# Two projection steps moved ahead of the first back step in even chunks of an mLSTM kernel

## The chip, the cores and the metric

The kernel runs on one core of a Trainium2 chip. The metric is the device time of one execution in microseconds (us). Before the change it is 3157.75 us, the median of three runs between 3157.44 and 3160.65 us.

The core's engines run side by side, each through its own queue in order: PE (matrix multiply, with PEld for its weight loads), DVE (vector), ACT (scalar), POOL (GpSimd) and SP, which here only issues transfers. They wait for each other through semaphores.

## The reference

One layer of a decoder: a norm, one input projection, two groups of heads that read the same projected input (a pooling mixer and an mLSTM), an output projection, a residual and a final norm. Width 1024, sequence 4096, all in float32. The change lies in the mLSTM branch, whose part that matters here is:

```python
xc = jax.nn.silu(causal_conv(mx, conv_w, conv_b))        # mx: a slice of u @ w_in, 1024 wide
q, k, v = headwise(xc, w_q), headwise(xc, w_k), headwise(mx, w_v)
gates = concatenate([q, k, v]) @ w_if + b_if             # input and forget gate of 4 heads
# chunks of 128 positions; (C, n, m) is carried from chunk to chunk
W = exp(d_log - m_t) * (q k^T)                           # within the chunk, causal
num = W v + inter * (C q);  den = sum(W) + inter * (n q)
h = num / max(|den|, exp(-m_t))
C_new = decay * C + sum(w * v k^T);  n_new = decay * n + sum(w * k)
```

## The kernel before

Every float32 matrix product that needs full precision is made of three products of a high and a low half: `split` (L109 to L111) makes the high half on ACT (L110) and the low half, the rest, on DVE (L111); `mm3` (L113 to L119) issues the three matmuls of each pair (L117 high by high, L118 high by low, L119 low by high). Lines L117 to L119 therefore stand for every such product, and the tile names tell them apart: `acc` in the mLSTM stage is the projection to `mx`.

The program has three stages: the norm and the pooling branch (L383 to L575), the mLSTM (L579 to L956), and the remaining projections (L961 on). In the middle one the sequence runs in 32 chunks of 128 positions, `n` = 0 to 31. Each turn of the loop at L935 takes the *front* of chunk n, the *back* of chunk n-1, and a share of the *projection* for a later block of 256 positions, which two chunks (an even and an odd one) share. All three are Python generators, and one `step` of a generator issues the instructions up to its next `yield`:

- `front` (L730), 13 steps: the v product from `mx` (three steps, L740), two steps for q (L750, copied by ACT at L752), two for the scores (L761), two transposes (L770), the gates (L774 to L785), the scans (L790 to L803), the split of a row into three bf16 parts (L812 to L815) and its spread over the partitions on PE (L817), and a last step with the exponentials (L820, L825, L829), the causal mask on POOL (L830), the product `dm` on DVE (L832), its split into `st` (called `wt` in the code, L833), and the scaled queries `qi` (L838 on DVE, L840 on ACT, L841 on POOL).
- `back` (L845), 13 steps with the preparing one: per head, the numerator from `st` (L867, three matmuls, of which the third needs the low half of `st`) and from the carried state (L871), the split of the state into `cs` (L643 on ACT, L644 on POOL), the division (L876 to L885), and two state updates (L896 on PE, L897 on DVE).
- `project` (L692): L702 and L703 split the four pieces of `u` on ACT and POOL; each of the 16 steps after that issues 12 matmuls (`proj_part`, L594), and each fourth step ends a pair of column groups: ACT copies `acc` to `mx` and scales it (L716, L721), POOL sets the three columns of overlap (L715, L717).

The pair's convolution is finished in pieces by `tail` (L651): six operations of DVE (L656), then the three activations of a SiLU (L678 to L680) and a product (L681). `acc` has a single PSUM buffer (L583), `mm` three, `map` four, the pieces of `u` twelve tiles (L580), `mx` five.

What is issued in which order comes from `ORDER` (L31): one string for even chunks and one for odd ones, with f for a step of the front, b of the back, p of the projection and c of a tail. This is the order of the program's text; the framework that places instructions on the engines keeps what depends on each other in order and may shift what doesn't, so the order on an engine is not that of the letters everywhere.

Of the kernel before, what the change touches and what calls it, by code (L numbers as in the profile page):

```python
# [27 lines left out]
TB = 256  # L28


ORDER = ("ffffbbffbpbffbpffppccbbbcbfpbfbbpppccc", "ffffbbbfpfffpbfbfppbccbbccfpbfpbppbbcc")  # L31
VA = P + 1
GW = P + 8

# [26 lines left out]
def tile_hybrid(  # L61
# [517 lines left out]
    with tc.tile_pool(name="b_one", bufs=1) as one, \  # L579
# [355 lines left out]
        for n in range(NB * NCH + 1):  # L935
            fr = Steps(front(n, n % 2, *xin), 13) if n < NB * NCH else None
            turn = {"f": fr, "b": bk, "p": proj}
            for what in ORDER[n % 2]:
                if what == "c":
# [275 lines left out]
```

## Time and profile before

| what | us |
|---|---|
| median of three runs | 3157.75 |
| the profiled execution, its time | 3153.02 |
| its span, first to last instruction | 3151.3 |
| PE busy with matmuls over the span | 2919.7 |
| DVE, ACT, POOL busy over the span | 2089.8, 1373.6, 960.7 |
| mean granted TensorE clock | 0.964 |

The page divides the span by lines and engines; a line such as L117 is met in all three stages, so the stages have to be looked at apart. The mLSTM stage begins at 767 us; its loop is in a steady rhythm from 873 to 1660 us, with one pair of chunks every 58.1 us. Times below are microseconds from the span's start. In a row of the timeline, the first number is the start, the second the time from the first to the last end of the instructions merged into the row, then engine, line, operation, tiles, and how many; brackets hold the idle time before it and what ended it.

### The profile page before, as it was taken

What the parts mean: (1) busy time and instruction counts of PE and PEld (TensorE: products, weight loads), DVE (VectorE), ACT (ScalarE), POOL (GpSimd) and SP (SyncE); (2) the same over time, 40 slices, a digit from 0 to 9 for tenths busy, and PEclk for the clock granted to TensorE, in tenths of its full rate; (3) what the DMA queues carried; (4) which work ended last, traced back from release to release, by engine and by line L of the source; (5) the groups of instructions that cost most, each with busy time, mean ns of one, the idle gap of its engine ahead of it and who ended that gap; (6) DMA issues with size and microseconds to landing.
All of it is one profiled execution on the core that took longest, in us unless ns stands there. A gap on an engine that the chain in (4) does not pass through costs nothing. (4 is left out here: it accounts for less than half of the span.)

```text
span 3151.3 us, 45085 instructions
## 1 busy us (share of the span) xinstructions
PE 2919.7 (93%) x15912; PEld 2522.1 (80%) x15912; DVE 2089.8 (66%) x4160; ACT 1373.6 (44%) x2727; POOL 960.7 (30%) x1015
## 2 busy tenths in 40 slices
PE   7999999996989999999997788999998899998998
PEld 6888888885989989989897566887777688876887
DVE  6555555544578878888888553566667766575666
ACT  4222122211577677767666311235556633342332
POOL 1122333333245455445445432001111145321000
PEclk9999999998899999999998899999999999998999
DMA  6344455556121121111113688765666788786654
GB/s 211 124 153 159 155 181 184 184 174 201 46 64 51 48 68 48 61 55 51 61 58 111 227 309 268 238 225 192 209 218 230 260 273 302 260 290 208 213 208 157
DMA packets 256419, 530.55 MB, mean 168 GB/s; under 512 B 28352, under 2 KB 71872, under 8 KB 256192
## 3 DMA queue, kind: packets, MB, share of 16 engines
q1 hardware_dynamic: 223936, 410.21, 37.6%
q10 hardware_dynamic: 32256, 117.45, 11.9%
q8 instruction: 125, 2.05, 0.3%
q14 instruction: 102, 0.84, 0.1%
HBM read 334.63 MB, written 192.94 MB: 167 GB/s over the span
## 5 line engine op out<-in xcount | busy, mean ns | idle before, releaser
L117 PE MATMUL acc<-u,w 128*128 128x512 f32 (+1 forms) x2016 | 691.6, 343 | 2.2 <-ACT u L110 1.8
L119 PE MATMUL acc<-u,w 128*128 128x512 f32 (+1 forms) x2016 | 682.4, 339 | 0.0
L118 PE MATMUL acc<-u,w 128*128 128x512 f32 (+1 forms) x2016 | 680.7, 338 | 0.0
L117 PE MATMUL ps<-w,sr 128*128 128x512 f32 x1344 | 536.7, 399 | 44.4 <-ACT sr L110 29.6
L119 PE MATMUL ps<-w,sr 128*128 128x512 f32 x1344 | 533.6, 397 | 9.2 <-DVE sr L111 9.0
L118 PE MATMUL ps<-w,sr 128*128 128x512 f32 x1344 | 532.5, 396 | 0.0
L111 DVE TENSOR_TENSOR sr<-sr 128x1024 fp32r<-128x1024 f32 x224 | 293.5, 1314 | 304.3 <-ACT sr L110 299.4
L110 ACT CAST sr<-sr 128x1024 fp32r<-128x1024 f32 x224 | 234.2, 1048 | 552.0 <-PE ps L118 293.6
L117 PEld LDWEIGHTS acc<-u,w 128*128 128x128 f32 x2016 | 383.7, 190 | 44.3 <-ACT u L110 2.5
L118 PEld LDWEIGHTS acc<-u,w 128*128 128x128 f32 x2016 | 383.7, 190 | 40.3
L119 PEld LDWEIGHTS acc<-u,w 128*128 128x128 f32 x2016 | 383.5, 190 | 40.2
L117 PEld LDWEIGHTS ps<-w,sr 128*128 128x128 f32 x1344 | 257.9, 192 | 99.6 <-ACT sr L110 32.3
L119 PEld LDWEIGHTS ps<-w,sr 128*128 128x128 f32 x1344 | 257.1, 191 | 69.5 <-DVE sr L111 16.7
L118 PEld LDWEIGHTS ps<-w,sr 128*128 128x128 f32 x1344 | 257.6, 192 | 53.5 <-issue 0.5
L656 DVE SCALAR_TENSOR_TENSOR xc<-mx,col,xc 128x256 f32<-128x256 f32 x384 | 221.2, 632 | 55.4 <-POOL mx L715 46.4
L644 POOL TENSOR_TENSOR cs<-c,cs 128x516 fp32r<-128x516 f32 x124 | 176.4, 1422 | 204.2 <-ACT cs L643 181.7
L1038 POOL TENSOR_TENSOR rs<-rs,nhalf 128x2 f32<-128x2 f32 x64 | 56.0, 876 | 521.0 <-DVE mv L1035 325.9
L117 PE MATMUL ps<-sr,w 128*128 128x512 f32 x448 | 176.5, 394 | 4.3 <-ACT sr L110 3.3
L118 PE MATMUL ps<-sr,w 128*128 128x512 f32 x448 | 176.0, 393 | 1.4 <-DVE sr L111 1.4
L119 PE MATMUL ps<-sr,w 128*128 128x512 f32 x448 | 175.7, 392 | 0.0
L867 PE MATMUL mm<-va,st 128*128 128x258 f32 x384 | 85.6, 318 | 64.2 <-DVE st L111 42.6
L322 DVE TENSOR_TENSOR ch<-ps,ch 128x512 f32<-128x512 f32 x192 | 127.2, 681 | 14.4 <-PE ps L119 13.6
(211 smaller groups left out, 5192.8 us busy)
## 6 DMA issues: line engine op xcount, KB each, us to landing
sr<-us_d ACTq DMA_DIRECT2D x112, 512.0 KB, 5.0
us_d<-st SPq DMA_DIRECT2D x64, 512.0 KB, 2.7
sr<-yp_d ACTq DMA_DIRECT2D x56, 512.0 KB, 5.3
sr<-ym_d ACTq DMA_DIRECT2D x56, 512.0 KB, 4.5
st<-in_x_t_dram SPq DMA_DIRECT2D x32, 512.0 KB, 6.1
yp_d<-sg SPq DMA_DIRECT2D x64, 256.0 KB, 2.5
st<-us_d SPq DMA_DIRECT2D x32, 512.0 KB, 5.8
st<-yp_d SPq DMA_DIRECT2D x32, 512.0 KB, 5.8
```

The costliest lines, as they stand in the source:

```text
L110: nc.scalar.copy(out=hi, in_=raw)
L111: (eng or nc.vector).tensor_tensor(out=lo, in0=raw, in1=hi.bitcast(F32), op=ALU.subtract)
L117: nc.tensor.matmul(ps, lhsT=a[0], rhs=b[0], start=start and k == 0, stop=False, skip_group_check=skip)
L118: nc.tensor.matmul(ps, lhsT=a[0], rhs=b[1], start=False, stop=False, skip_group_check=skip)
L119: nc.tensor.matmul(ps, lhsT=a[1], rhs=b[0], start=False, stop=stop and k == n - 1, skip_group_check=skip)
L322: nc.vector.tensor_tensor(out=v(t), in0=ps, in1=v(t), op=ALU.add)
L644: nc.gpsimd.tensor_tensor(out=t[:, 1], in0=cst[h], in1=t[:, 0].bitcast(F32), op=ALU.subtract)
L656: nc.vector.scalar_tensor_tensor(out=a[:, t], in0=m[:, t, i:i + TB], scalar=conv_w[:, jj * 4 + i:jj * 4 + i + 1], in1=a[:, t], op0=ALU.mul ...
L867: nc.tensor.matmul(nps, lhsT=wt[:, w, h, :], rhs=vh[v], start=i == 0, stop=first and i == 2)
L1038: nc.gpsimd.tensor_tensor(out=rs, in0=rs, in1=nhalf[:, 0:2], op=ALU.pow)
```

## The change

One of the two strings changes, that for even chunks. Two steps of the projection now come directly after the first four of the front, before the first of the back; in exchange the one between the third and fourth step of the back goes, and of the three at the end, two are left. The sum of letters is the same, and the string for odd chunks is not touched.

```diff
-ORDER = ("ffffbbffbpbffbpffppccbbbcbfpbfbbppppccc", "ffffbbbfpfffpbfbfppbccbbccfpbfpbppbbcc")
+ORDER = ("ffffppbbffbbffbpffppccbbbcbfpbfbbppccc", "ffffbbbfpfffpbfbfppbccbbccfpbfpbppbbcc")
```

On the engines this moves instructions in three places, the same in every pair of the steady rhythm.

The first is PE at the head of an even chunk, from the front's first q product on (`map`: the front; `mm`: the back; `acc`: the projection). Before:

```order
L750 MATMUL map<-xc,bqk 128x128 x4
L867 MATMUL mm<-va_11209,st 128x258
L867 MATMUL mm<-va_11210,st 128x258
L896 MATMUL mm<-va_11209,ws 128x258
L896 MATMUL mm<-va_11210,ws 128x258
L896 MATMUL mm<-va_11209,ws 128x258
L896 MATMUL mm<-va_11210,ws 128x258
L117 MATMUL acc<-u,w_5551 128x256
L118 MATMUL acc<-u,w_5551 128x256
L867 MATMUL mm<-va_11209,st 128x258
L871 MATMUL mm<-cs,qi 128x258 x6
```

With the change 18 matmuls of the projection stand between the q product and the first L867 (12 with the weights w_5551 and w_5552, then six with w_5553 and w_5554, of which the last are shown):

```order
L119 MATMUL acc<-u,w_5552 128x256
L117 MATMUL acc<-u,w_5553 128x256
L118 MATMUL acc<-u,w_5553 128x256
L119 MATMUL acc<-u,w_5554 128x256
L117 MATMUL acc<-u,w_5553 128x256
L118 MATMUL acc<-u,w_5553 128x256
L119 MATMUL acc<-u,w_5554 128x256
L867 MATMUL mm<-va_11209,st 128x258
L867 MATMUL mm<-va_11210,st 128x258
L867 MATMUL mm<-va_11209,st 128x258
L871 MATMUL mm<-cs,qi 128x258 x6
```

So the third L867, the one that needs the low half of `st`, moved from behind four matmuls of the state update and two of the projection to behind 18 of the projection.

The second is DVE later in the even chunk, where the row is split into three bf16 parts for PE's L817. Before, nothing stands between the pieces of the split:

```order
L799 TENSOR_TENSOR brow<-brow,mt 4x128
L812 CAST parts_5629<-brow 4x128
L813 TENSOR_TENSOR rows<-brow,parts_5629 4x128
L814 CAST parts_5629<-rows 4x128
L815 TENSOR_TENSOR parts_5629<-rows,parts_5629 4x128
L897 SCALAR_TENSOR_TENSOR c_5714<-c_5714,decay,mm 128x258
L656 SCALAR_TENSOR_TENSOR xc<-mx,col,xc 128x256
```

With the change the last piece, L815, comes after a pair's six convolution operations and two state updates of the back (one more update, of c_5714, and L813 stand just ahead of these rows):

```order
L656 SCALAR_TENSOR_TENSOR xc<-mx,col,xc 128x256
L814 CAST parts_5629<-rows 4x128
L656 SCALAR_TENSOR_TENSOR xc<-mx,col,xc 128x256 x4
L854 SCALAR_TENSOR_TENSOR ws<-st,wcol,ws 128x256
L656 SCALAR_TENSOR_TENSOR xc<-mx,col,xc 128x256
L876 SCALAR_TENSOR_TENSOR r<-mm,expm 128x1
L897 SCALAR_TENSOR_TENSOR c_5715<-c_5715,decay,mm 128x258
L878 TENSOR_TENSOR r<-mm,r 128x1
L897 SCALAR_TENSOR_TENSOR c_5715<-c_5715,decay,mm 128x258
L879 RECIPROCAL r<-r 128x1
L808 COPY ibc<-map 128x4
L815 TENSOR_TENSOR parts_5629<-rows,parts_5629 4x128
```

The third is DVE where the odd chunk begins, at the product `dm` and the low half of `st` that the odd chunk's back reads. Before:

```order
L832 TENSOR_TENSOR dm<-sc,dm 128x512
L854 SCALAR_TENSOR_TENSOR ws<-st,wcol,ws 128x256 x2
L111 TENSOR_TENSOR st<-dm,st 128x512
L656 SCALAR_TENSOR_TENSOR xc<-mx,col,xc 128x256 x6
L111 TENSOR_TENSOR va_11210<-map,va_11209 128x3x128
```

With the change the six L656 of the next pair have moved ahead of the low half of `st`:

```order
L832 TENSOR_TENSOR dm<-sc,dm 128x512
L656 SCALAR_TENSOR_TENSOR xc<-mx,col,xc 128x256 x6
L111 TENSOR_TENSOR st<-dm,st 128x512
L854 SCALAR_TENSOR_TENSOR ws<-st,wcol,ws 128x256 x2
L111 TENSOR_TENSOR va_11210<-map,va_11209 128x3x128
```

At the head of the odd chunk PE's order has moved too: eleven matmuls of the projection and four of the state update now stand between its second and third L867, which were neighbours before. On ACT the copy of the second pair of scores (L763) now stands behind a state split (L643), a numerator's scaling (L885) and a split of `u` (L702).

More of the change, by code (lines that the diff above doesn't have):

```diff
@@ L28 @@
 TB = 256
-ORDER = ("ffffbbffbpbffbpffppccbbbcbfpbfbbpppccc", "ffffbbbfpfffpbfbfppbccbbccfpbfpbppbbcc")
+ORDER = ("ffffppbbffbbffbpffppccbbbcbfpbfbbppccc", "ffffbbbfpfffpbfbfppbccbbccfpbfpbppbbcc")
 VA = P + 1
```

## The prediction

> **What bounds the kernel now.** I read the page's head first, then the busy times by stage, then PE's waits in the mLSTM stage, then the timeline of one pair of chunks on each engine.
>
> ```profile
> span 3151.3 us, 45085 instructions
> core 0: us, PE busy (x) PEld busy (x) DVE busy (x) ACT busy (x) POOL busy (x), PEclk, DMA share, GB/s
> 820.00:1690.00 870.00, 802.25 (x6495) 778.76 (x6494) 704.85 (x1948) 610.14 (x1479) 414.81 (x524) 0.97 0.18 59
> 1221.37:1279.43 58.06, 54.07 (x442) 52.56 (x441) 47.50 (x133) 41.21 (x102) 28.52 (x37) 0.97 0.17 55
> ...
> engine line waited for: us in total, times, longest us
> PE mm L867 <- DVE st L111: 39.7, 14, 2.9
> ```
>
> In the loop PE is busy for 802 of 870 us, DVE for 705, and transfers take 18% of the DMA engines. A pair of chunks (the last row of the windows) takes 58.06 us, 54.07 of them with PE busy. PE sets the pace, and nearly all that is left is one wait of PE, met 14 times, once in each pair: the third L867 of the even chunk's back, for the low half of `st`.
>
> ```profile
> 1191.55 0.28 PE L117 MATMUL acc<-u,w 128*128 128x256 f32 x1
> ...
> 1194.93 0.28 PE L119 MATMUL acc<-u,w 128*128 128x256 f32 x1
> ...
> 1223.22 1.05 PE L750 MATMUL map<-xc,bqk 128*128 128x128 f32 x8
> 1224.03 0.48 PE L867 MATMUL mm<-va,st 128*128 128x258 f32 x2
> ...
> 1228.09 0.58 PE L867 MATMUL mm<-va,st 128*128 128x258 f32 x1 [2.86 <-DVE st L111]
> ...
> 1231.37 0.36 PE L119 MATMUL acc<-u,w 128*128 128x256 f32 x1
> ...
> 1238.91 0.27 PE L784 MATMUL map<-ident,lf 128*4 128x128 f32 x1 [0.45 <-DVE lf L781]
> ...
> 1228.00:1228.50 0.50, 0.41 (x2) 0.41 (x3) 0.50 (x3) 0.50 (x3) 0.00 (x0) 0.50 0.00 0
> 1231.00:1231.50 0.50, 0.50 (x6) 0.50 (x5) 0.50 (x5) 0.30 (x1) 0.50 (x1) 0.81 0.14 53
> ...
> 1221.19 1.22 DVE L832 TENSOR_TENSOR dm<-sc,dm 128x512 f32<-128x512 f32 x1 [1.71 <-POOL dm L830]
> ...
> 1223.12 4.31 DVE L656 SCALAR_TENSOR_TENSOR xc<-mx,col,xc 128x256 f32<-128x256 f32 x6
> 1227.36 0.68 DVE L111 TENSOR_TENSOR st<-dm,st 128x512 fp32r<-128x512 f32 x1
> ```
>
> A matmul of the back or the projection costs 0.117 us from start to start (30 from 1191.55 on, 3.5 us), one of L750 0.10. PE stands still for 2.86 us because DVE does six convolution operations, 4.31 us, between `dm` and the low half of `st`. The granted clock then falls to 0.50 until about 1231.3: from 1228.09 to 1231.37 PE does 12 such matmuls and four of L750, 1.8 us at the full clock, in 3.28. Wait and slow clock together are 2.86 + 1.48 = 4.3 us a pair, 61 us in 14 pairs: the most the change could take out here.
>
> **The change, part by part.** The count of matmuls stays as it is; only waits can change. I follow one pair from 1221.37, with the clock full.
>
> *Even chunk, head.* What must the 18 matmuls moved up wait for?
>
> ```profile
> 1224.08 0.65 ACT L702 CAST u<-u 128x512 fp32r<-128x512 f32 x1
> 1227.46 0.63 ACT L678 ACTIVATE sgm<-xc 128x512 f32<-128x512 f32 x1 [2.35 <-DVE xc L656]
> 1229.67 0.62 ACT L702 CAST u<-u 128x512 fp32r<-128x512 f32 x1
> ...
> 1224.85 1.51 POOL L703 TENSOR_TENSOR u<-u 128x512 fp32r<-128x512 f32 x1
> 1230.37 1.28 POOL L703 TENSOR_TENSOR u<-u 128x512 fp32r<-128x512 f32 x1 [4.01 <-ACT u L702]
> ```
>
> These two pairs of rows make the third and fourth piece of `u` (the first two are a chunk old). PE leaves L750 at 1224.03 and does 13 matmuls until 1225.55. The 14th needs POOL's third piece, 1226.36: 0.8 us of waiting; five more bring 1226.95. Two L867 follow, and the third still waits for DVE until 1228.09 (0.9 us), as nothing on DVE has moved ahead of it. After L871, at 1228.93, the 19th matmul needs the fourth piece from ACT. That stands behind the SiLU that waits for the same six L656, and ends at 1230.29: 1.4 us; its low half comes at 1231.65: 0.6 us more. So one wait of 2.86 us becomes four that sum to 3.7; what goes is the slow clock, and what is done meanwhile is projection.
>
> Up to L784, 12 matmuls more than before are then done, 1.40 us of PE. L784 itself comes later:
>
> ```profile
> 1234.98 0.62 ACT L643 CAST cs<-c 128x516 fp32r<-128x516 f32 x1
> 1235.51 0.47 ACT L885 ACTIVATE ht<-mm,r 128x256 f32<-128x256 f32 x1
> 1235.88 0.36 ACT L763 COPY sc<-map 128x256 f32<-128x256 f32 x1
> ```
>
> The gates need the second L763, which now stands behind L643, L885 and L702. L643 has to wait for the second head's L871, which adding up puts at 1235.2; with L643, L885 and a transfer of 0.15 us between engines, then L702, L763 ends at 1237.1 instead of 1236.2. DVE and ACT follow as before, and L784 starts at about 1239.9, 1.0 later. Gain: 1.4 - 1.0 = **0.4 us**. The bounds are 1.4 (the gates not late) and -0.6 (a further us late); I take the middle, as it is a sum of rows.
>
> *Even chunk, end.* L817 waits for L815, which has gone behind the convolution.
>
> ```profile
> 1240.83 0.28 DVE L799 TENSOR_TENSOR brow<-brow,mt 4x128 f32<-4x128 f32 x1
> 1241.96 0.28 DVE L815 TENSOR_TENSOR parts<-rows,parts 4x128 bf16<-4x128 f32 x1
> ...
> 1243.68 3.10 DVE L656 SCALAR_TENSOR_TENSOR xc<-mx,col,xc 128x256 f32<-128x256 f32 x5
> ...
> 1245.89 0.40 PE L817 MATMUL map<-parts,sel 68*128 68x128 bf16 x4
> ...
> 1247.35 0.58 ACT L820 ACTIVATE inter<-map 128x512 f32<-128x512 f32 x1
> ...
> 1250.15 0.88 ACT L829 ACTIVATE dm<-map,ibc 128x128 f32<-128x128 f32 x3
> ```
>
> With L784 1.0 later, L799 ends at 1242.1. Behind it stand six L656 (0.62 each), one L854 and three L897 (some 0.45), and seven small ones (0.15): 6.6 us, so L815 ends at 1248.7 instead of 1242.2. PE has L867 and L871 of the last head ahead of L817 and meets it there, at 1249.1 instead of 1246.3. PE itself loses nothing by that yet: it ends the even chunk 0.4 us earlier than 1253.13, at 1252.7.
>
> *Odd chunk, head.* What hung on L817 is late now.
>
> ```profile
> 1251.82 0.83 POOL L830 TENSOR_SCALAR_AFFINE_SELECT dm<-dm 128x512 f32<-128x512 f32 x1
> 1252.62 2.75 POOL L841 TENSOR_TENSOR qi<-qr,qi 128x256 fp32r<-128x256 f32 x3
> 1255.31 0.99 POOL L715 COPY mx<-mhal 128x6 f32<-128x6 f32 x2
> ...
> 1255.58 0.68 DVE L111 TENSOR_TENSOR st<-dm,st 128x512 fp32r<-128x512 f32 x1
> 1256.18 2.45 DVE L656 SCALAR_TENSOR_TENSOR xc<-mx,col,xc 128x256 f32<-128x256 f32 x6
> ...
> 1253.13 2.02 PE L740 MATMUL map<-bvg,mx 128*128 128x136 f32 x16
> 1254.99 1.05 PE L750 MATMUL map<-xc,bqk 128*128 128x128 f32 x8
> 1255.80 0.90 PE L867 MATMUL mm<-va,st 128*128 128x258 f32 x3
> ```
>
> Before, L830 starts 5.5 us after L817, with parts of a SiLU and of other work between on ACT. These now lie ahead of L820; what remains between, L820, one L885 and four L829, is 2.1 us (0.5, 0.4 and 1.2). I take 3.9, near the middle of the two: L830 at 1253.0. It and three L841 last until 1256.5, and only then comes L715, for which the first of the six L656 waits: they start at 1257.0. They last 2.45 us (POOL on copies) to 4.31 (POOL on tensor operations); I take 2.85, one at 0.7 and five at 0.43. The low half of `st` then ends at **1260.4**, where before it ended at 1256.26, ahead of the convolution. PE, from 1252.7, has 1.86 us of L740, 0.81 of L750, two L867 and the 15 matmuls now in front of the third: 1257.4. It waits **3.0 us**, where before it waited for nothing (bounds 1.2 with 2.1 us in place of the 3.9, and 6.1 with 5.5 there and L656 at 4.31). The low halves of the front's `va` are late with it and hold up L750 and L761 by some **0.5 us** (0 to 1).
>
> *The clock.* The slow phase of the even chunk is in the 1238.91 that I compared with. If the odd head's wait brings one, it costs up to 1.48; its 3.0 us are broken by hoisted matmuls. I take half, **0.7** (0 to 1.48 at each of two heads). [...]
>
> *Sum.* -0.4 + 3.0 + 0.5 + 0.7 = 3.8 us a pair; 14 pairs, 53 us. The first chunk and the last two, where the steps load weights instead, keep their order around `st`; I take them at nothing (2 us either way). The profiled execution takes 3153.0 us, 1.7 of it outside the span: 3206. The median lies 4.7 above that execution: **3211 us**.
>
> **The rivals.**
>
> *The projection fills the wait and the odd chunk holds* (faster). For it: 18 matmuls do stand where PE stood still, and the odd head has 15 in front of its third L867. It decides at the odd head: if L815 to L111 takes 8.7 us or less, not the 11.7 summed above, `st` is ready by 1257.4 and there is no wait. With the gates on time too, each pair gains 1.4 us: -20, 3138. Against it: three L841 alone are 2.75 us of that chain, and the six L656 at least 2.45. Chance 0.15.
>
> *No change*: the odd wait is about what the even one gave, 0.4 to 0.8 a pair; 3158 to within 6 us, which is 0.2%, about what a measurement of this kernel can tell from no change. Chance 0.07.
>
> *Both heads wait, both cold* (slower still). The even head's four waits leave PE busy for about a third of the time from 1227 to 1230.4, which may suffice for a slow phase, and L656 may take 4.31 beside POOL's last L841. That adds 0.7 + 1.5 + 1.5 a pair to the forecast, 52 us: 3263. Chance 0.13.
>
> *The order on the engines doesn't follow the letters.* It follows on PE at the even head; where DVE departs from them is the forecast's very reason. No chance of its own.
>
> **How the numbers follow.** The forecast has 0.65, with its own range from 1.8 us a pair (3183) to 5.5 (3235). Faster by over 0.2% is 0.15, within it 0.07, slower 0.78 (forecast and third rival). The range from 3150 to 3245 leaves out most of the first rival and about half of the third, some 0.2.
>
> **What would show it.** In the changed profile: no wait of 2.86 us for `st` in even chunks but shorter ones for L702, L703 and L111; L817 some 9 us after L784, where it was 7.0; in odd chunks a wait of PE's L867 for `st` L111, 14 times, of 2 to 4 us, and DVE's L656 waiting for POOL's L715 ahead of it; a pair of 61 to 62 us in place of 58.1. I am wrong if odd chunks show no such wait, or if the even head keeps a single long one.

## The result and the profile after

The changed kernel takes 3193.74 us, the median of four runs (3193.3 to 3194.68), beside 3157.6 us before on the same chip: a ratio of 1.0113, with a 95% interval of 1.0096 to 1.0131. The profiled execution took 3193.3 us, 1.8 of them outside the span.

Two things told ahead need a correction. In the diff quoted there the removed line has one p too many; before the change the even string ends in `bbpppccc`. And by the program's text the tails do stand ahead of `st`: the string holds 12 of the front's 13 steps, and the last, with `dm` and `st`, is issued by `finish` (L949) when the whole string is through. It was before the change that the framework had shifted `st` in front of the convolution in odd chunks; with the change it doesn't.

First the head of the page of the changed kernel, its windows for the loop's stretch and for one pair (from the even head, the first L740 of the even chunk, to the next: span, busy time with instructions for PE, PEld, DVE, ACT and POOL, granted clock, DMA share, GB/s), and PE's waits from 820 to 1720 us (total, times, longest).

```profile
span 3191.5 us, 45058 instructions
```

```profile
820.00:1690.00 870.00, 787.17 (x6279) 751.07 (x6278) 664.76 (x1875) 589.71 (x1421) 369.75 (x499) 0.98 0.17 54
1055.53:1115.59 60.06, 54.14 (x442) 51.62 (x441) 46.77 (x133) 41.40 (x102) 26.75 (x37) 1.00 0.17 54
```

```profile
engine line waited for: us in total, times, longest us
PE mm L867 <- DVE st L111: 28.1, 27, 1.5
PE acc L117 <- ACT u L702: 16.6, 15, 1.2
PE acc L118 <- POOL u L703: 14.5, 28, 1.1
PE map L784 <- DVE lf L781: 10.8, 14, 0.9
...
PE mm L867 <- ACT st L110: 4.3, 14, 0.3
```

The pair has the same 442 instructions on PE and 54.14 us of work instead of 54.07; it lasts 60.06 us instead of 58.06, though at the full clock. The one wait of 2.86 us has gone. In its place PE waits for `u` on two engines, for the gates longer than before, and for `st` in both chunks. In the next fence, the timeline of PE in that pair (start, time, instruction; in brackets the idle time before it and what ended it), the four waits of the even head come first, then those of the odd head, which starts at 1087.09.

```profile
1055.53 2.02 PE L740 MATMUL map<-bvg,mx 128*128 128x136 f32 x16
...
1060.58 0.39 PE L118 MATMUL acc<-u,w 128*128 128x256 f32 x1 [0.61 <-POOL u L703]
...
1062.25 0.39 PE L867 MATMUL mm<-va,st 128*128 128x258 f32 x1 [0.57 <-DVE st L111]
...
1064.51 0.39 PE L117 MATMUL acc<-u,w 128*128 128x256 f32 x1 [1.16 <-ACT u L702]
...
1065.87 0.39 PE L118 MATMUL acc<-u,w 128*128 128x256 f32 x1 [0.38 <-POOL u L703]
...
1074.08 0.27 PE L784 MATMUL map<-ident,lf 128*4 128x128 f32 x1 [0.76 <-DVE lf L781]
...
1083.27 0.40 PE L817 MATMUL map<-parts,sel 68*128 68x128 bf16 x4
...
1087.09 2.01 PE L740 MATMUL map<-bvg,mx 128*128 128x136 f32 x16
1088.94 1.05 PE L750 MATMUL map<-xc,bqk 128*128 128x128 f32 x8
1090.30 0.50 PE L867 MATMUL mm<-va,st 128*128 128x258 f32 x2 [0.31 <-ACT st L110]
...
1092.34 0.28 PE L118 MATMUL acc<-u,w 128*128 128x256 f32 x1
1094.10 0.39 PE L867 MATMUL mm<-va,st 128*128 128x258 f32 x1 [1.48 <-DVE st L111]
```

And the other engines at the odd head, from the timelines of DVE, ACT and POOL:

```profile
1082.63 0.28 DVE L815 TENSOR_TENSOR parts<-rows,parts 4x128 bf16<-4x128 f32 x1
...
1087.87 1.21 DVE L832 TENSOR_TENSOR dm<-sc,dm 128x512 f32<-128x512 f32 x1 [0.91 <-POOL dm L830]
1090.52 2.92 DVE L656 SCALAR_TENSOR_TENSOR xc<-mx,col,xc 128x256 f32<-128x256 f32 x6 [1.44 <-POOL mx L715]
1093.37 0.68 DVE L111 TENSOR_TENSOR st<-dm,st 128x512 fp32r<-128x512 f32 x1
...
1084.19 0.60 ACT L820 ACTIVATE inter<-map 128x512 f32<-128x512 f32 x1
...
1088.21 0.61 ACT L716 COPY mx<-acc 128x512 f32<-128x512 f32 x1
1088.68 1.06 ACT L721 ACTIVATE xc<-acc,col 128x256 f32<-128x256 f32 x2
1089.59 0.65 ACT L110 CAST st<-dm 128x512 fp32r<-128x512 f32 x1
...
1087.20 0.64 POOL L830 TENSOR_SCALAR_AFFINE_SELECT dm<-dm 128x512 f32<-128x512 f32 x1 [1.20 <-ACT dm L829]
1087.80 2.55 POOL L841 TENSOR_TENSOR qi<-qr,qi 128x256 fp32r<-128x256 f32 x3
1090.30 0.19 POOL L715 COPY mx<-mhal 128x6 f32<-128x6 f32 x1
```

This is a late chain from end to end: L817 starts 3.8 us ahead of the odd head (1087.09 - 1083.27; before 7.2), `dm` ends 2.0 us after it (1089.08; before, 0.8), then DVE stands still for 1.44 us because the first L656 in its queue needs POOL's L715, which stands behind three L841, and only after the six L656 comes the low half of `st`.

All odd chunks and all even chunks have the same matmuls, so their lengths from head to head can be compared between all kernels here. Over the 12 pairs of the steady rhythm from `n` = 4 to 27:

| | even chunk, mean (least to most) | odd chunk, mean | pair |
|---|---|---|---|
| before | 31.78 (31.69 to 31.91) | 26.31 | 58.09 |
| after | 32.40 (31.53 to 33.22) | 28.48 | 60.88 |

The odd chunk loses 2.17 us every time. The even chunk, where before the clock fell in every pair, is 0.2 us shorter when the clock stays full (31.56 against 31.78), and longer where it falls, as it still does in 9 of the 14 from `n` = 2 to 28. A pair loses 2.79 us, the 12 pairs 33.5 us. With the first pair, which gains 0.9, and the last, which loses 1.6, the 14 pairs lose 34.1 us. The two profiled executions differ by 40.3: the other 6.2 us lie ahead of these pairs (2.6) and behind them (3.6), and no experiment follows them.

### The profile page after: what moved, and what is told of

Same layout as the page of the kernel before. It is cut to its first block, busy times and chain, and to the rows that moved or that the text cites. A ratio compares the mean times of both kernels' runs of the same rounds, so it can differ in the third digit from the quotient of the medians.

```text
span 3191.5 us, 45058 instructions
## 1 busy us (share of the span) xinstructions
PE 2931.5 (92%) x15912; PEld 2521.0 (79%) x15912; DVE 2084.5 (65%) x4160; ACT 1376.8 (43%) x2727; POOL 934.2 (29%) x1015
## 5 line engine op out<-in xcount | busy, mean ns | idle before, releaser
L110 ACT CAST sr<-sr 128x1024 fp32r<-128x1024 f32 x224 | 234.2, 1048 | 551.5 <-PE ps L118 278.5
L656 DVE SCALAR_TENSOR_TENSOR xc<-mx,col,xc 128x256 f32<-128x256 f32 x384 | 232.0, 658 | 72.9 <-POOL mx L715 67.3
L644 POOL TENSOR_TENSOR cs<-c,cs 128x516 fp32r<-128x516 f32 x124 | 165.8, 1337 | 335.0 <-ACT cs L643 312.5
L897 DVE SCALAR_TENSOR_TENSOR c<-c,decay,mm 128x258 f32<-128x258 f32 x248 | 115.2, 471 | 54.9 <-PE mm L896 53.2
L546 DVE TENSOR_TENSOR sum<-z 128x527 f32<-128x527 f32 x64 | 64.8, 1013 | 120.4 <-ACT z L534 120.2
```

The source lines that it names most:

```text
L110: nc.scalar.copy(out=hi, in_=raw)
L546: nc.vector.tensor_tensor(out=nxt[:, a:], in0=cur[:, a:], in1=cur[:, a - step:HALO + T - step], op=ALU.add)
L644: nc.gpsimd.tensor_tensor(out=t[:, 1], in0=cst[h], in1=t[:, 0].bitcast(F32), op=ALU.subtract)
L656: nc.vector.scalar_tensor_tensor(out=a[:, t], in0=m[:, t, i:i + TB], scalar=conv_w[:, jj * 4 + i:jj * 4 + i + 1], in1=a[:, t], op0=ALU.mul ...
L897: nc.vector.scalar_tensor_tensor(out=cst[h][:, t], in0=cst[h][:, t], scalar=decay[:, h:h + 1], in1=upd, op0=ALU.mult, op1=ALU.add)
```

## The experiments

Two questions stood: is it the step taken from the even chunk's end that costs, and is it then the late chain from L815 to `dm`, or the convolution that stands ahead of `st`? All ratios are to the kernel before on the same chip, with 95% intervals. Each edit changes the strings of L31 alone; where one line is shown, it is the even string, and the odd one is that of before.

**One step alone.** The first takes only the middle step to the head, the second only the one from the end.

```diff
-"ffffbbffbpbffbpffppccbbbcbfpbfbbpppccc"
+"ffffpbbffbbffbpffppccbbbcbfpbfbbpppccc"   (middle)
+"ffffpbbffbpbffbpffppccbbbcbfpbfbbppccc"   (end)
```

> Even string ffffpbbffbbffbpffppccbbbcbfpbfbbpppccc: only the step from between the third and fourth back step moves to the front, the three at the end stay. On DVE the parts L812 to L815 stay together and the odd chunk's low half of st (L111) stays ahead of the six L656, as before the change. Theory (the loss comes from DVE's order at the odd head and from the late L815, both brought by the step taken from the end): no wait of L867 for st in odd chunks; in even chunks 12 matmuls ahead of the first L867 and a shorter wait for st of about 2.4 us in place of 2.86; 3130 to 3155 us, I take 3148. Rival (the loss comes from filling the even head, that is from the waits for u and what they make late): part of the loss is here already, 3165 to 3180.

> Even string ffffpbbffbpbffbpffppccbbbcbfpbfbbppccc: only the step from the end moves to the front. DVE's order is that of the change: L815 behind six L656, and six L656 ahead of the odd chunk's st. Theory: odd chunks wait as with the change (0.3 us for ACT's half and about 1.5 us for DVE's half of st), even chunks have 12 matmuls in the gap and no wait for u; 3170 to 3195 us, I take 3183. Rival (the loss comes from filling the even head): with one step there, without a wait for u, 3150 to 3165.

Middle step: 3147.26 us, ratio 0.9983 (0.9973 to 0.9994). The wait for `st` at the even head is shorter by 0.7 us, the odd chunk takes 26.32 us and waits for nothing. End step: 3175.7 us, ratio 1.0072 (1.0052 to 1.0091). PE's waits of the latter from 820 to 1720 us:

```profile
PE mm L867 <- DVE st L111: 52.1, 28, 3.3
...
PE mm L867 <- ACT st L110: 4.2, 14, 0.3
```

28 waits for `st`, two in each pair, and the 14 short ones for ACT: the odd chunk takes 28.48 us, to 0.01 what it takes with both steps moved. So, in these strings, the whole loss of the odd chunk comes with the step from the end. The even chunk shows what the second step at the head is worth: with the end step alone it takes 30.78 us at the full clock, with both 31.56. The first twelve matmuls fit into the wait. The next six need pieces of `u` that are only then being made, and bring three waits of 0.61, 1.16 and 0.38 us for a shorter one for `st`. That is the larger part of why the two steps don't add up: moved singly, a pair changes by -0.46 and by +1.76 us, moved together by +2.79 (means of the same 12 pairs).

**`st` first in the odd chunk.** The front's last step is written into the string, ahead of the tails. On DVE the low half of `st` then follows `dm` at once; L815, L817 and `dm` stay late.

```diff
-"ffffppbbffbbffbpffppccbbbcbfpbfbbppccc"   (the change)
+"ffffppbbffbbffbpffppccbbbcbfpbfbbfppccc"
```

> The changed kernel with one f more in the even string, ahead of the last two p: ffffppbbffbbffbpffppccbbbcbfpbfbbfppccc, so that the front's last step is issued ahead of the last tail. DVE's order is then L832, L111 of st, and only behind them the six L656; L815 stays as late as with the change. Theory that the six L656 ahead of st make the odd wait: the wait for st falls from 1.8 us to 0.4 or less, 3160 to 3175 us, I take 3168. Rival that the late L815 makes it alone: the wait stays over 1 us, 3185 to 3195.

3181.94 us, ratio 1.0091 (1.0072 to 1.0110): in neither range, and nearer to the rival. The odd chunk takes 28.17 us, only 0.31 less, or 4 us in 14 pairs. The rest of the difference to the changed kernel isn't the odd head's: the clock fell in only 2 of the 14 even chunks of this profiled execution, whose heads have the same waits. PE's timeline has, in one odd chunk:

```profile
1088.90 2.01 PE L740 MATMUL map<-bvg,mx 128*128 128x136 f32 x16
...
1092.79 0.39 PE L867 MATMUL mm<-va,st 128*128 128x258 f32 x1 [0.67 <-DVE st L111]
...
1096.19 0.51 PE L896 MATMUL mm<-va,ws 128*128 128x258 f32 x2 [0.87 <-DVE ws L854]
```

A wait for `st` is left, and a second one came, for `ws`, which now stands behind the same six L656.

**`st` first in the even chunk**, on the kernel before, by an f in place of a b in the odd string (the back's missing step is then issued behind the string): does taking the convolution out of the way of `st` bring the even chunk's 2.86 us?

```diff
-"ffffbbbfpfffpbfbfppbccbbccfpbfpbppbbcc"   (odd)
+"ffffbbbfpfffpbfbfppbccbbccfpbfpfppbbcc"   (odd)
```

> The kernel before the change with the even string untouched and one f more in the odd string: ffffbbbfpfffpbfbfppbccbbccfpbfpbfppbbcc. DVE then makes the low half of st, on which PE waited 2.86 us at the even head, ahead of the six L656. Theory (DVE's order makes the waits at both heads; but the six L656 and the SiLU behind them must still end before the even chunk's second L750): the wait for st goes, a smaller one for L681 or L750 takes its place, no slow clock at the even head in most pairs; 3120 to 3150 us, I take 3138. Rival (PE only moves its wait to L750 and loses the same there): 3152 to 3163.

3157.9 us, ratio 1.0014 (1.0000 to 1.0027): the rival's time, though the wait did not go to L750. PE's waits show where it went:

```profile
PE mm L896 <- DVE ws L854: 42.2, 15, 2.9
PE map L784 <- DVE lf L781: 18.5, 13, 1.5
```

The wait for `st` is gone, and one for `ws` of the same 2.9 us stands in its place; the gates are late by a further us.

**An earlier L815**, without and with `st` first. Here the middle tail goes behind a step of the front, so that L815 no longer stands behind all six L656.

```diff
-"ffffppbbffbbffbpffppccbbbcbfpbfbbppccc"   (the change)
+"ffffppbbffbbffbpffppbbbbfpbfcccbbppccc"   (earlier split)
+"ffffppbbffbbffbpffppbbbbfpbfcccbbfppccc"  (earlier split, st first)
```

> The changed even string with the three steps of the middle tail (c) and one step of the front (f) exchanged in its second half, so that on DVE two convolution operations instead of six, and no third state update, stand ahead of the last piece of the row's split (L815); the six convolution operations of the next pair still stand ahead of the low half of st in the odd chunk. Theory after the run that put st first (the late L815, and with it L817, dm and st, makes some 1.9 of the odd chunk's loss of 2.17 us, the convolution ahead of st 0.3): odd chunk 26.6 us from head to head instead of 28.48, 14 x 1.9 = 26 us less than the changed kernel, ratio to the kernel before about 1.003 (1.000 to 1.006). Rival (the convolution ahead of st is enough by itself): odd chunk 28 us or more, ratio 1.008 to 1.012.

> As the run with the earlier split, and the front's last step one letter earlier, so that the low half of st directly follows dm in the odd chunk: both of the suspected causes are gone. Theory: odd chunk 26.3 us as before the change, no wait for st in either chunk over 1 us; the even chunk as in the changed kernel (31.5, or 32.5 where the clock falls): ratio 0.997 to 1.003. Rival (the loss comes from the projection's matmuls that moved from the even chunk's end into its head, whatever DVE does): odd chunk over 27.5 us, ratio over 1.006.

Neither expectation's theory held. 3202.26 us, ratio 1.0149 (1.0132 to 1.0166), and 3205.08 us, 1.0162 (1.0148 to 1.0176): slower than the change itself. The rivals' lower bounds are passed too, but by a cause that neither names. The timelines of DVE, ACT and PE in the first of them, at an odd head that lies at 1086.31, show it:

```profile
1080.26 0.28 DVE L815 TENSOR_TENSOR parts<-rows,parts 4x128 bf16<-4x128 f32 x1
...
1083.32 0.63 ACT L678 ACTIVATE sgm<-xc 128x512 f32<-128x512 f32 x1 [2.01 <-DVE xc L656]
1083.98 0.63 ACT L679 ACTIVATE sgm<-sgm 128x512 f32<-128x512 f32 x1
...
1085.92 0.58 ACT L820 ACTIVATE inter<-map 128x512 f32<-128x512 f32 x1
...
1082.49 0.40 PE L817 MATMUL map<-parts,sel 68*128 68x128 bf16 x4
...
1090.96 0.51 PE L867 MATMUL mm<-va,st 128*128 128x258 f32 x2 [1.35 <-ACT st L110]
...
1093.81 0.39 PE L867 MATMUL mm<-va,st 128*128 128x258 f32 x1 [0.45 <-DVE st L111]
```

L815 now ends 1.95 us ahead of L817 (0.36 in the changed kernel), and L817 starts 3.82 us ahead of the odd head, as in the changed kernel. So L817 wasn't held by L815 there: its place on PE holds it, 30 matmuls ahead of the head, 51 before the change. And on ACT the activations of the moved tail (L678 to L680) now wait and run between L817 and L820, so that `dm` ends 3.5 us after the odd head (4.0 with `st` first) instead of 2.0. The odd chunk takes 29.65 us (29.6 with `st` first and at the full clock).

**Two candidates for a faster kernel.** The odd string's last p one b later, with the middle step at the even head and without it:

```diff
-"ffffbbffbpbffbpffppccbbbcbfpbfbbpppccc", "ffffbbbfpfffpbfbfppbccbbccfpbfpbppbbcc"
+"ffffpbbffbbffbpffppccbbbcbfpbfbbpppccc", "ffffbbbfpfffpbfbfppbccbbccfpbfppbpbbcc"
+"ffffbbffbpbffbpffppccbbbcbfpbfbbpppccc", "ffffbbbfpfffpbfbfppbccbbccfpbfppbpbbcc"
```

> A candidate that leaves the even chunk's end alone: of the changed even string only the middle step is moved to the head, and in the odd string the last p comes two letters later, behind the second b of its group, while the p before it comes earlier (...fppbpbbcc instead of ...fpbppbbcc), so that on DVE the six convolution operations finish ahead of dm instead of between dm and the low half of st at the even head. Theory: the wait of 2.2 us for st at the even head goes, and with it the slow clock of some 1.5 us a pair; at least 1.5 us a pair less: ratio 0.985 to 0.994. Rival (the wait moves to another tile of the same queue, as it did to ws in the run with st first in the even chunk; here dm itself would come later by the six operations): ratio 0.997 to 1.003.

> The even string as before the change, the odd string as in the candidate: does the candidate's gain need the moved step at all? If the six convolution operations between dm and st are the whole cause of the even head's wait: no wait for st, ratio 0.985 to 0.995 and within 0.003 of the candidate. Rival (it needs twelve matmuls of projection at the head to bridge the rest): a wait for st of 1 us or more stays and the candidate is faster by over 0.003.

The first: 3149.21 us, ratio 0.9981 (0.9972 to 0.9991). The second: 3154.5 us, ratio 1.0001 (0.9992 to 1.0010). In both the wait for `st` goes and one for `ws` comes, of 1.2 us with the twelve matmuls at the head and 2.6 without. For the first that is the rival, in its ratio and in the move of the wait, though `dm` comes earlier, not later (0.2 us after the even head; before, 1.0), and shorter waits for L716, L752 and L681 join it. The second fits neither text: no wait for `st` is left, which the rival wanted, and the ratio is above the theory's. The first is faster by 0.002, not by over 0.003.

**Two steps at the head, L817 earlier on PE.** Three strings with both steps at the head, the rest of the even string rearranged.

```diff
-"ffffppbbffbbffbpffppccbbbcbfpbfbbppccc"   (the change)
+"ffffppbbffbbffbffppbccbbbcbfpbfbpppccc"   (fill kept, cover)
+"ffffppbbffbbffbffppccbbbcbfpbfbbpppccc"   (three at the end)
+"ffffppbbffbffbpffppccbbbcbfpbbfbbppccc"   (the third)
```

> Both steps stand at the head of the even chunk as in the changed kernel, but the steps behind it are put so that 42 matmuls, not 30, stand on PE between L817 and the odd chunk's head (51 before the change), and that the low half of st follows dm at once in the odd chunk. Theory after the two runs with the earlier split (not the place of L815 on DVE decides, but how far ahead of the odd head L817 stands on PE, since all of L817, L820, L829, L830, L832 and st has to fit into that stretch): L817 starts 5.3 us ahead of the odd head (3.8 in the changed kernel, 7.2 before), dm ends 0.5 to 1.5 us after it (2.0 and 0.8), the odd chunk takes 26.3 to 26.8 us, and the ratio is 0.996 to 1.003. Rival (18 matmuls of projection at the even head cost the odd chunk its work, wherever L817 stands): odd chunk 28 us or more, ratio 1.006 or more.

> Both steps at the even head, taken from the two single p between the back's steps; three p stay at the end of the even string. By the letters the odd chunk's cover is that of before, yet on PE 33 matmuls stand between L817 and the odd head, because the framework puts the row's split behind the convolution here too. Theory (the matmuls between L817 and the head decide, not the letters at the string's end): L817 4.2 us ahead of the odd head, dm 1.6 after it, a wait for st in every odd chunk, odd chunk 27.5 to 28.4 us, ratio 1.004 to 1.010. Rival (the step taken from the end is the cause, as the two runs with one step each seemed to say): odd chunk 26.3 to 26.6, ratio below 1.001.

> Both steps at the even head, 35 matmuls between L817 and the odd head, and st directly behind dm in the odd chunk: between the changed kernel with st first (30 matmuls, odd chunk 28.2) and the run with 42. Theory: L817 4.5 us ahead of the odd head, dm ends 1.3 to 1.6 us after it, odd chunk 26.5 to 27.5 us, ratio 0.999 to 1.006. Rival (late L815 on DVE costs by itself, since it stands behind six L656 and three L897 here as in the changed kernel): odd chunk 28 us or more, ratio over 1.008.

In the first and the third of these the premise of the expectation didn't hold. In their traces 34 and 30 matmuls stand between L817 and the odd head, not 42 and 35, and the six L656 stand ahead of `st` in both, so they don't test what they were meant to. They give two more points: 3201.95 us, ratio 1.0154 (1.0137 to 1.0170), odd chunk 28.23; and 3172.62 us, 1.0062 (1.0047 to 1.0077), odd chunk 28.15. Their odd chunks are nearly alike; what parts them is the even chunk, 32.74 and 31.35 us. The second is as it was described, with 33 matmuls: 3187.14 us, ratio 1.0108 (1.0090 to 1.0125), odd chunk 27.92, with a wait for `st` of 1.46 us in every odd chunk. Three p at the end don't save it; the rival fails, and the theory's 27.5 to 28.4 us hold for the odd chunk, its ratio not quite (the even chunk takes 32.33 us).

**The convolution out of the way of `ws` too.** As with `st` first in the odd chunk, and the last tail moved into the odd string:

```diff
-"ffffppbbffbbffbpffppccbbbcbfpbfbbfppccc", "ffffbbbfpfffpbfbfppbccbbccfpbfpbppbbcc"
+"ffffppbbffbbffbpffppccbbbcbfpbfbbfpp", "ffffbbbfcccpfffpbfbfppbccbbccfpbfpbppbbcc"
```

> The kernel with st first in the odd chunk, and in addition the last tail of the even string (three c) moved into the odd string, where it is the same work one step later: on DVE the low half of st directly follows dm, and only two convolution operations instead of six stand ahead of the two ws (L854). The even chunk, L815 and L817 stay as in the changed kernel, so dm is as late as there (2.0 us after the odd head, 0.8 before). Theory A (the late dm costs one short wait, 0.67 us plus 0.16 for the restart of PE; the rest of the odd chunk's 2.17 us is the convolution, first ahead of st, then ahead of ws): odd chunk 26.9 to 27.4 us, ratio 1.002 to 1.006. Theory B (the late L815 and L817, and so dm, make most of it, about 1.9 us): odd chunk 28 us or more, ratio 1.008 or more.

3187.09 us, ratio 1.0098 (1.0072 to 1.0124), odd chunk 28.14 us: theory B's number. PE's timeline in one odd chunk:

```profile
1087.85 0.39 PE L867 MATMUL mm<-va,st 128*128 128x258 f32 x1 [0.67 <-DVE st L111]
...
1089.67 0.75 PE L896 MATMUL mm<-va,ws 128*128 128x258 f32 x4 [0.47 <-DVE ws L854]
...
1090.72 1.13 PE L750 MATMUL map<-xc,bqk 128*128 128x128 f32 x8 [0.18 <-DVE part L743]
```

Only two L656 are left ahead of `ws`, and the odd chunk still loses 1.83 us, now at three places: whatever stands next in DVE's queue behind the late `dm` is late. With `dm` at 2.0 us the order behind it is worth 0.3 us; with `dm` at 3.5 to 4.0 the odd chunk loses 3.3.

Over the kernels of these runs, in the order of the second column, the odd chunk goes with the time at which `dm` ends, and, where that is 2.0 us or later, only weakly with what stands behind it:

| | `dm` ends after the odd head | L656 between `dm` and `st` | odd chunk |
|---|---|---|---|
| before, and middle step alone | 0.8 | none | 26.3 |
| three at the end | 1.27 | six | 27.92 |
| the third of those strings | 1.48 | six | 28.15 |
| fill kept, cover | 1.74 | six | 28.23 |
| after, and end step alone | 2.0 | six | 28.48 |
| `st` first in the odd chunk | 2.0 | none | 28.17 |
| convolution out of the way of `ws` | 2.0 | none | 28.14 |
| earlier split | 3.5 | six | 29.65 |
| earlier split, `st` first | 4.0 | none | 29.6 at the full clock |

What the runs leave open: the six L656 ahead of `st` aren't innocent either. With 33 matmuls behind L817 `dm` ends only 1.27 us after the head, and 1.6 us are lost. On a straight line through the rows without L656 between, 26.3 at 0.8 and 28.17 at 2.0, that `dm` would give some 27.0 us; by this estimate the six L656 cost 0.9 there, more than the 0.3 at 2.0. No kernel was run that has `dm` as early as before and the convolution ahead of `st` in the odd chunk, so how much each of the two costs alone at an early `dm` isn't known; they overlap. Nor is `dm` set by PE's distance alone: with the same 30 matmuls behind L817 it ends 1.48, 2.0, 3.5 or 4.0 us after the head, as the work of ACT between L817 and L829 differs. Nor did any order tried keep both steps at the head and L817 where it was.

## Why the prediction held, and where its sum was off

The forecast was 3211 us, slower, by an odd chunk that waits; it came out slower, at 3194, by an odd chunk that waits. Counted from the even head of the pair:

- *Even head, four waits in place of one.* Forecast 0.8, 0.9, 1.4 and 0.6; measured 0.61, 0.57, 1.16 and 0.38, in this order and by these releasers. Right; the forecast counts from start to start, where each is some 0.16 longer than its bracket. The run with the end step alone shows the same from the other side: the second step meets unfinished `u`.
- *L784 1.0 us later.* Forecast 18.5 after the head, measured 18.55 (1074.08 - 1055.53), against 17.54 before. Right; PE's wait there rose from 0.45 to 0.76. On the way, the step from PE's L871 to ACT's L643, for which the forecast has 0.15 us, took 0.09 by the modelled end of the matmul (1068.88 + 0.88 to 1069.85). The gain of 0.4 us in the chunk was 0.2 at the full clock.
- *L817 27.7 us after the even head, L830 at 31.6.* L817 started at 27.74 and L830 at 31.67. That L830 fits so well is luck. The 1246.3 of before, with which the forecast compares its 27.7, is the end of L817 (1245.89 + 0.40), and by its end L817 came at 28.14. From there to L830 it was 3.5 us, where the forecast took 3.9, the middle of two bounds, and ACT still had an L680 and an L643 ahead of L820 and a wait of 0.73 us behind it. Of the reason, the run with the earlier split shows that PE's place for L817, which the prediction mentions only beside L815, is the one that counts: an L815 that ends earlier moves nothing.
- *The convolution waits for L715 ahead of `st`.* Right: the bracket of 1.44 us is that wait, and L656 starts 35.0 after the head (forecast 35.6: L830 and three L841 took 3.1 us rather than 3.5, and the first L715 0.19 rather than half of 0.99).
- *The wait for `st`, 3.0 us: the term that was mis-sized.* Measured 1.48 us, or 1.64 from start to start as the forecast counts, with 0.31 for ACT's half ahead of it; the sign told ahead was 2 to 4 us. `st` ended at 38.5, not 39.0. PE came 0.9 later, ready for the third L867 at 36.9 rather than 36.0: its odd head was 0.2 later, the first L867 started 0.5 later because it had to wait for ACT's L110, which stands behind L716 and two L721, and the 17 matmuls from there took 0.2 more. That ACT wait wasn't in the prediction.
- *Late `va`, 0.5 us.* Not there: no wait of PE for L743 in the odd chunk. With the 3.0 above, 3.5 us were forecast for the odd chunk, and 2.17 came.
- *The clock, 0.7 us.* Measured 0.84 a pair (mean of the even chunk 32.40 against 31.56), but at the even head, where the third rival had it, and never at the odd one. That the size fits is luck.
- *The sum.* 3.8 us a pair forecast, 2.79 measured in the steady pairs, and 34.1 instead of 53 us over the 14. What lies outside them, taken at nothing, was 6.2 us longer. The 4.7 us put on top for the median weren't there (profiled 3193.3, median 3193.74). Less by 19, more by 6 and less by 4 make up the 17 us.
- *The rivals.* The first needed `st` at 36.0 after the head and got 38.5. The fourth was told imprecisely, as said above: at the odd head DVE follows the text after the change and departed from it before.

The experiments corrected one thing in my reading of the cause: I took the convolution ahead of `st` for the larger part, and the runs with `st` first show that the late `dm` alone is enough for 1.8 to 1.9 of the 2.17 us. As for a version better than both, the middle step alone (0.9983) and the same with the odd string's later p (0.9981) are the best found, a gain of about 0.2% with intervals that end below 1.

## What to carry to other kernels

Work that stands at the end of an iteration may be the cover under which the next one's first operands are made; ask what runs beside it before taking it to fill a wait elsewhere, and count the distance on the waiting engine (here 51 matmuls against 30) and the work of every engine that the operand passes on its way, not only the place on the engine that makes it. A wait named after one tile often belongs to a queue: in five runs here `st` was brought forward, and all of the wait or part of it went to `ws`, the next tile behind it. Filling a wait pays up to the point at which the filler's own inputs are ready, here one step of two.

## What the runs showed of the hardware

The odd head's wait cost PE more than the idle time in its bracket. The 1.48 us lie between a start at 1092.34 and one at 1094.10; a running series would have started at 1092.46, so 1.64 us are lost, 0.16 more. The bracket counts from the end of the matmul before, and matmuls' ends are modelled in the profile, here 0.28 us behind the start, so the 0.16, which the expectation of the last experiment puts down to a restart of PE, say how a bracket is to be read. The starts by themselves show a little more: the matmul behind the one that waited, an L871, starts 0.22 us after it, at 1094.32, where a running series has 0.117. Over the odd chunk two waits of 1.79 us in sum cost 2.17, and in the last experiment three of 1.32 cost 1.83.

In the changed kernel the clock fell without one long wait. Two windows of half a microsecond in another even head:

```profile
1005.00:1005.50 0.50, 0.50 (x5) 0.50 (x4) 0.00 (x0) 0.37 (x1) 0.44 (x2) 0.50 0.79 238
1007.00:1007.50 0.50, 0.50 (x4) 0.50 (x4) 0.00 (x0) 0.37 (x1) 0.00 (x0) 0.50 0.00 0
```

PE is busy in both and gets half the clock. Such phases of 3.41 us (this one from 1004.41 to 1007.82) came in 9 of 14 even heads, behind waits of at most 1.2 us with matmuls between them; before the change they came in all 14 (the first of 6.83 us), behind one wait of 2.86. Even heads with the same waits were hit in some pairs and spared in others, and the run with `st` first in the odd chunk, with these waits too, was hit in 2 of 14.

What decides between them the traces don't show. In the changed kernel the phases at 942.97, 1004.41 and 1185.32 us begin 61.44 and 180.91 us apart, 18 and 53 times the length of one phase, and the other six, too, lie whole multiples of it apart. In the step of this grid just ahead of a phase PE was busy for 49 to 56% by the profile's count; in the five spared heads the emptiest step had 55 to 64%. These are the step ahead of the phase at 1004.41, and one in the spared head at 1055.53 with the step behind it:

```profile
1001.00:1004.41 3.41, 1.86 (x13) 1.46 (x12) 3.28 (x12) 2.81 (x7) 1.55 (x2) 1.00 0.14 47
1062.44:1065.85 3.41, 1.89 (x13) 1.50 (x12) 3.35 (x12) 3.02 (x7) 1.32 (x2) 1.00 0.08 27
1065.85:1069.26 3.41, 3.39 (x29) 3.39 (x30) 0.70 (x3) 2.44 (x5) 2.49 (x2) 1.00 0.46 129
```

PE is busy for 1.86 and for 1.89 us, 55% in both, and only the first was followed by half the clock. In this kernel, then, filling a wait with work that has to wait itself kept the clock in 5 of 14 pairs and not in the others.
